# Attention stage of a decoder layer: the eight PSUM banks divided as five, two and one instead of four, two and two

## The chip, the cores and the metric

One core of a Trainium2 chip runs the whole kernel. The metric is the device time of one execution in microseconds; the median over the runs is compared. Of an execution taken by the hardware profiler there is also a trace with every instruction of every engine.

## What is computed

One decoder layer on a sequence of 2048 tokens of width 1024, in float32. The attention part, cut to what matters here:

```python
# banded heads: 8 query heads on 2 key heads of 64, window of 128 keys, a sink per head
out_a = sliding_window_sink_attention(qa, ka, va, sinks)
# differential heads: 4 heads, two causal softmax maps each, values of width 128
p = softmax(where(mask, q @ k.T * scale, -inf))      # for both maps c = 0, 1
a = p[:, :, 0] - lam * p[:, :, 1]
od = a @ v
out_b = rms_norm(od, g_diff) * (1.0 - lam_init)
x = x + concat(out_a, out_b) @ w_out
```

In front of it stand an RMS norm and one combined projection; behind it cross-attention to 256 memory tokens and a squared-ReLU MLP with 4096 hidden columns.

## The kernel before, in words

The layer is written as stages that follow each other: `phase_in` (norm, projections, rotary tables, L215), `phase_attention` (L435), `phase_out` (output projection, L768), then cross-attention (L813 to L1003) and the MLP (L1070 to L1218). Matrix products that need more than one pass split each float32 operand into a high and a low part and take three products.

The kernel uses PSUM as eight banks of 128x512 float32 values. `K.ps` (L87) takes a bank by a tag, and `BANKS` (L52) says how many buffers a tag has: four for `s`, two for `t`, two for `o`. One PSUM pool (L1246) serves the whole kernel. A tile keeps its bank until its last reader is done; the next tile of the tag waits for that.

The attention stage has four kinds of work, all in `phase_attention`.

- *Scores and exponentials of a unit* (`softmax`, L454). A unit is one differential head `h` and a block `s` of 256 queries: 4 heads by 8 blocks, 32 units. Keys are taken 512 at a time; for each such chunk and each half of the queries two maps are made. Two matmuls (L482) fill a bank of tag `s` (a third, L487, adds the causal mask in the last chunk), VectorE takes the negated row maximum (L488), ScalarE the exponential with that bias (L489) into an SBUF tile `p`. The exponential is the last reader of the bank.
- *Weighting* (`weigh`, L498). Small operations make each chunk's factors (L506 to L516). GpSimd multiplies the second map (L521), and VectorE computes first map times factor plus second (L528); for some tiles GpSimd does this too (L523, L524).
- *Values of a unit* (`values`, L533). For each 256 keys four transposes (L553) fill a bank of tag `t`. ScalarE copies it (L560), or ScalarE and VectorE split it into a high and a low part (L141, L142). Then matmuls with the values (L543) add into one bank of tag `o` that the unit holds from its first to its last matmul. At the end ScalarE copies it out (L571), GpSimd squares it (L572), and a sum over the partitions goes through a bank of tag `t` (L576, L578).
- *Banded heads* (`window_softmax`, L599, and `window_values`, L637). 32 pieces, each with two score banks of tag `s` (L611, read by L622 to L627), one bank of tag `t` for transposes (L643, L645), and one of tag `o` for the output `wo` (L657 to L663): two matmuls, and a copy by ScalarE.

Beside these, 16 columns of the memory's projection (`memory_column`, L752) run as filling: 24 matmuls into a bank of tag `t` and a split.

The order is written as a plan of times (L668 to L714). Each unit gets a start and a duration, from `U0` and `U1`; its score, weighting and value steps get planned times from `W0`, `W1` and `VL`. All steps are sorted by planned time and issued in that order (L713). A unit's value steps are planned behind its scores, by a formula (L693, L694) that takes no notice of the other units; where a unit follows a longer one, its first value step can be planned ahead of the last one's end. The units run over the blocks upward in heads 0 and 2 and downward in heads 1 and 3 (L39, L668). The program is built with a scheduler (L1328) that, per engine, puts an instruction whose inputs and buffers are there by its model ahead of one that still waits, with the written order as the priority; on the chip each engine then runs that fixed order.

The PSUM pool, like the SBUF pools, is opened with `reuse_waits="tile"` (L1241): a new tile waits for the earlier tiles at its place. The SBUF pool `work` (L1250) already takes over in this way the place of a pool that `phase_in` closes.

Of the kernel before, what the change touches and what calls it, by code (L numbers as in the profile page):

```python
# [9 lines left out]
F32 = mybir.dt.float32  # L10
# [7 lines left out]
P = 128  # L18
S = 2048
D = 1024  # L20
NT = S // P
# [15 lines left out]
W0, W1, VL, WS, WV = 2.0, 1.0, 4.0, (0.42, 0.6, 0.92), (0.33, 0.86)  # L37
# [11 lines left out]
AHEAD, WOUT = 3, 28  # L49

MAIN, STAGE, SLAB, W2, WIN, W2O = 36, 6, 4, 8, 5, 3
BANKS = dict(s=4, t=2, o=2)  # L52


SPLIT = ((1, 0, 1, 0, 1, 0, 1, 0), (1, 1, 1, 0, 1, 1, 1, 0), (1, 0, 0, 1, 0, 0, 1, 0))
# [2 lines left out]
def f(t):  # L58
    return t.bitcast(F32)
# [6 lines left out]
class K:  # L66
# [18 lines left out]
        return self.work_pool.tile(list(shape), dtype, name=name, tag="out", bufs=W2O)  # L85

    def ps(self, tag, shape=(P, 512), name="ps"):  # L87
        return self.psum_pool.tile(list(shape), F32, name=name, tag=tag, bufs=BANKS[tag])

    def bank(self, i, name="ps"):  # L90
        return self.ps("ssssttoo"[i], name=name)
# [111 lines left out]
def constants(k, pool):  # L203
    nc = k.nc
    k.ident = pool.tile([P, P], F32, name="ident")
    make_identity(nc, k.ident)
    k.identb = pool.tile([P, P], BF16, name="identb")
    nc.scalar.copy(k.identb, k.ident)
    k.gv = pool.tile([P, 48], F32, name="gv")
    k.load(k.gv, k.a["gvec"])  # L210
    k.g_mix, k.g_cross, k.g_mem, k.g_mlp, k.g_final = (k.gv[:, 8 * i : 8 * i + 8] for i in range(5))
    k.g_diff, k.inv_freq, k.sgn, k.qk_scale = (k.gv[:, 40 + i : 41 + i] for i in range(4))
# [222 lines left out]
def phase_attention(k, mt):  # L435

    nc = k.nc
    kv, sw, started, turned = {}, {}, {}, []
# [198 lines left out]
    def window_values(cc, g, b, p):  # L637

        vs = sw[cc, g][2]
        blk = 2 * cc + b  # L640
        tt = k.ps("t", [P, 4, P], name="wtt")
        for j in range(4):
            nc.tensor.transpose(tt[:, j, :], p[:, j], k.ident)  # L643
        a1 = k.win([P, 4, P], name="wa1")
        nc.scalar.copy(a1, tt)  # L645
        parts = [(b + 1, a1)]
        if blk:
            a0 = k.win([P, 4, P], name="wa0")
            nc.gpsimd.affine_select(
                out=a0, in_=a1, compare_op=ALU.is_ge, fill=0.0, base=-1, pattern=[[0, 4], [-1, P]], channel_multiplier=1  # L650
            )
            nc.gpsimd.affine_select(
                out=a1, in_=a1, compare_op=ALU.is_ge, fill=0.0, base=0, pattern=[[0, 4], [1, P]], channel_multiplier=-1
            )
            parts = [(b, a0), (b + 1, a1)]
        yield
        o = k.ps("o", [64, 512], name="wo")  # L657
        for x, (i, t) in enumerate(parts):
            nc.tensor.matmul(  # L659
                o, vs[:, i, :], t.rearrange("p a b -> p (a b)"), start=(x == 0), stop=(x == len(parts) - 1)  # L660
            )
        os_ = k.w2o([64, 4, P], name="wos")
        nc.scalar.copy(os_.rearrange("p a b -> p (a b)"), o)  # L663
        cs = slice(P * (blk % 4), P * (blk % 4) + P)
        nc.sync.dma_start(k.ow_d[blk // 4][:, 64 * g : 64 * g + 64, cs].rearrange("t f k -> f t k"), os_)
        yield
# [5 lines left out]
    def at(times, make, *args):  # L672

        state = []

        def step():
            if not state:
                state.append(make(*(y for x in args for y in (x[0] if isinstance(x, list) else (x,)))))
            return next(state[0], None)

        steps.extend((t, len(steps) + n, step) for n, t in enumerate(times))

    start = 0.0
    for i, (h, s) in enumerate(units):
        n, dur = (s + 2) // 2, U1 * (s + 1) + U0
        res = []

        def scores(h, s, i=i, res=res):
            yield from softmax(i, h, s, res)

        at([start + dur * (x + 0.5) / (2 * n) for x in range(2 * n)] + [start + dur * (1 - 0.1 / n)], scores, h, s)
        start += dur
        stt = [start + W0 + W1 * dur * (x + 1) / (2 * n) for x in range(2 * n)]  # L693
        val = [stt[2 * (x // 2) + 1] + VL + 0.5 * W1 * dur * (x % 2) / n for x in range(s + 1)]  # L694
        at([start] + stt, weigh, res)
        at(val + [val[-1] + VL, val[-1] + VL + 0.1], values, res)
    each = start / 32
    for i, win in enumerate(wins):
        res = []
# [44 lines left out]
def memory_load(k):  # L744
    mt = [[k.main([P, 4, MEM], name="mt") for _ in range(2)] for _ in range(2)]
    for y in range(2):
        for x in range(2):
            k.load(f(mt[x][y]), k.mt_d[x][y], chain="main")
    return mt
# [63 lines left out]
def cross_queries(k):  # L813

    nc, a = k.nc, k.a
    kk = [[k.main([P, 4, MEM], name="kk") for _ in range(2)] for _ in range(2)]
    for i in range(2):
        for x in range(2):
            k.load(f(kk[i][x]), k.kv_d[x][i], chain="main")
    wq = [[k.main(name="wq") for _ in range(2)] for _ in range(DT)]  # L820
    for h in range(4):
        pq = [k.bank(d, name="pq") for d in range(DT)]
        for e in range(2):
            w = k.slab2(a["w_cqT"][(2 * h + e) * P : (2 * h + e + 1) * P, :], "vector" if e else "gpsimd", h % 2 == 1)
            n = 2 * h + e
            for d in range(DT):
                for z, (s_, m_) in enumerate(((0, 0), (0, 1), (1, 0))):
                    nc.tensor.matmul(  # L828
                        pq[d][:, :256], w[s_][d // 4][:, P * (d % 4) : P * (d % 4) + P], kk[n // 4][m_][:, n % 4], start=(e == 0 and z == 0), stop=(e == 1 and z == 2)
                    )  # L830
        hs = slice(256 * h, 256 * h + 256)
        for d in range(DT):
            k.split(wq[d][0][:, hs], wq[d][1][:, hs], pq[d][:, :256], k.g_cross[:, d : d + 1])
    return wq
# [235 lines left out]
def phase_up(k, operands, rb, last_rstd):  # L1070
# [3 lines left out]
    def pair(half, n, sets, mid):  # L1074
# [23 lines left out]
        def add(ps, x, name, tile=k.w2):  # L1098
            t = tile(name=name)
            nc.vector.tensor_tensor(t, ps, x, op=ALU.add)  # L1100
            return t
# [119 lines left out]
def build(nc, tc, a, out):  # L1221
    k = K()
    k.last_load = {}
    k.nc, k.tc, k.a, k.out = nc, tc, a, out
    with ExitStack() as es:
        dp = es.enter_context(tc.tile_pool(name="dram", bufs=1, space=bass.MemoryType.DRAM))
        dram = lambda name, *shape: dp.tile(list(shape), F32, name=name)
        k.qk_d = [dram(f"qk_d{n}", 4 if n < 6 else 2, 2, HD, S) for n in range(7)]
        k.v_d = dram("v_d", 4, P, NT, 2 * P)
        k.vs_d = dram("vs_d", P, NT, P)  # L1230
        k.cs_d = dram("cs_d", 2, 32, S)
        k.ow_d, k.od_d = ([dram(f"{n}{i}", 4, P, 512) for i in range(4)] for n in ("ow_d", "od_d"))
        k.ss_d = [dram(f"ss_d{i}", 4, 512) for i in range(4)]
        k.rs_d = [dram(f"rs_d{i}", 1, 4, 512) for i in range(4)]
        k.kv_d = [[dram(f"kv_d{x}{i}", P, 4, MEM) for i in range(4)] for x in range(2)]
        k.mt_d = [[dram(f"mt_d{x}{i}", P, 4, MEM) for i in range(2)] for x in range(2)]
        k.t_d = [{n: dram(f"t_d{i}{n}", 2, 2, P, 512) for n in ("t1", "t2", "t3", "t4")} for i in range(2)]
        k.u_d = [[dram(f"u_d{c}_{n}", 2, P, 512) for n in range(16)] for c in range(4)]
        k.x1_d, k.x2_d = ([dram(f"{n}{c}", DT, P, 512) for c in range(4)] for n in ("x1_d", "x2_d"))

        pool = lambda name, **kw: es.enter_context(tc.tile_pool(name=name, bufs=1, reuse_waits="tile", **kw))  # L1241
        cp = pool("const")
        k.tiny_pool = pool("tiny")
        k.main_pool = pool("main")
        k.stage_pool = pool("stage")
        k.psum_pool = pool("psum", space=bass.MemoryType.PSUM)  # L1246
        constants(k, cp)
        k.rs1 = cp.tile([P, NT], F32, name="rs1")
        phase_in(k, cp)
        k.work_pool = pool("work")  # L1250
        started = phase_attention(k, memory_load(k))
        phase_out(k, started[WOUT])
        pt, last = cross_scores(k, cross_queries(k))
        vw = cross_values(k, last)
        operands = {}, {}
        make = mlp_operands(k, 0, operands[0])
        rb, last_rstd = cross_mix(k, pt, vw, lambda: [*mlp_combine(k, 0)], lambda: [next(make) for _ in range(4)])
        for _ in make:
            pass
        phase_up(k, operands, rb, last_rstd)  # L1260
        phase_down(k)
# [77 lines left out]
```

## Time and profile before

| | |
|---|---|
| median of 3 runs | 3046.49 us (3045.34 to 3056.3) |
| the profiled execution | 3047.63 us |
| its span, first to last instruction | 3045.6 us |
| granted TensorE clock, mean | 0.974 of full speed |
| busy share of the span | TensorE matmul 95%, weight load 77%, VectorE 58%, ScalarE 37%, GpSimd 38% |

How to read it: the profile page gives each engine's busy share over the whole span, and that mixes stages. Every part of the argument on the attention stage needs rows of that stage alone: busy time in a window, waits in that window, instructions in order of time. A wait is put down to the instruction that released it. Clock 1.00 is the 2.4 GHz level, 0.50 the 1.2 GHz level.

### The profile page before, as it was taken

What the parts mean: (1) busy time and instruction counts of PE and PEld (TensorE: products, weight loads), DVE (VectorE), ACT (ScalarE), POOL (GpSimd) and SP (SyncE); (2) the same over time, 40 slices, a digit from 0 to 9 for tenths busy, and PEclk for the clock granted to TensorE, in tenths of its full rate; (3) what the DMA queues carried; (4) which work ended last, traced back from release to release, by engine and by line L of the source; (5) the groups of instructions that cost most, each with busy time, mean ns of one, the idle gap of its engine ahead of it and who ended that gap; (6) DMA issues with size and microseconds to landing.
All of it is one profiled execution on the core that took longest, in us unless ns stands there. A gap on an engine that the chain in (4) does not pass through costs nothing.

```text
span 3045.6 us, 38727 instructions
## 1 busy us (share of the span) xinstructions
PE 2884.5 (95%) x13740; PEld 2350.0 (77%) x13740; DVE 1760.0 (58%) x2918; ACT 1125.9 (37%) x2481; POOL 1163.8 (38%) x914
## 2 busy tenths in 40 slices
PE   8999989989999899999995999989999999999996
PEld 8978866666666688888883877878888888888886
DVE  5254448887788642423345756665556566656656
ACT  7221137666767422444223333433342111111113
POOL 0133336765676542112124666665561101110115
PEclk9999989989999999999997999999999999999997
DMA  8443363434432664211327345443346122212203
GB/s 310 133 178 126 111 197 115 121 84 140 126 109 81 196 208 138 84 42 66 108 90 276 124 148 170 145 154 111 111 139 228 63 76 77 77 63 77 77 7 111
DMA packets 223297, 380.21 MB, mean 125 GB/s; under 512 B 25313, under 2 KB 95105, under 8 KB 223105
## 3 DMA queue, kind: packets, MB, share of 16 engines
q1 hardware_dynamic: 223104, 377.75, 37.5%
q8 instruction: 108, 1.77, 0.2%
q14 instruction: 85, 0.69, 0.1%
HBM read 259.65 MB, written 116.98 MB: 124 GB/s over the span
## 4 chain that ended last, share of the span: by engine, by line
PE 61%; DVE 5%; DMA 4%; POOL 4%; issue 2%; ACT 1%; SPq 0%; POOLq 0%; DVEq 0%; ACTq 0%
PE pd L1179 23%; PE p L1093 15%; PE po L804 6%; PE sc L868 6%; PE po L992 5%; PE sc L482 1%; DMA xs<-x_d 1%; DVE p L528 1%; PE o L543 1%; POOL w L1089 1%; PE wo L659 1%; DMA wf<-w_up 1%; PE pv L934 1%; PE pq L828 1%; POOL p L521 1%
## 5 line engine op out<-in xcount | busy, mean ns | idle before, releaser
L1093 PE MATMUL p<-xh,w 128*128 128x512 f32 x1792 | 557.3, 392 | 42.9 <-ACT w L1088 27.6
L1183 DVE TENSOR_TENSOR acc<-pd,acc 128x512 f32<-128x512 f32 (+1 forms) x520 | 351.2, 681 | 253.7 <-PE pd L1179 251.2
L1093 PEld LDWEIGHTS p<-xh,w 128*128 128x128 f32 x1792 | 337.0, 189 | 121.3 <-ACT w L1088 29.6
L1179 PE MATMUL pd<-uh,wdh 128*128 128x512 f32 (+1 forms) x1040 | 401.7, 386 | 1.0 <-DVE acc L1183 1.0
L1179 PE MATMUL pd<-ul,wdh 128*128 128x512 f32 (+1 forms) x1040 | 401.2, 386 | 0.0
L1179 PE MATMUL pd<-uh,wdl 128*128 128x512 f32 (+1 forms) x1040 | 401.2, 386 | 0.0
L1093 PE MATMUL p<-xl,w 128*128 128x512 f32 x896 | 350.3, 391 | 0.0
L117 POOL TENSOR_TENSOR wdl<-wf,wdh 128x1024 fp32r<-128x1024 f32 x32 | 78.0, 2440 | 549.6 <-ACT wdh L116 543.8
L489 ACT ACTIVATE p<-sc,nm 128x512 f32<-128x512 f32 (+3 forms) x320 | 198.8, 627 | 95.9 <-DVE nm L488 94.3
L482 PE MATMUL sc<-kt,q 128*128 128x512 f32 (+2 forms) x640 | 199.1, 414 | 32.0 <-ACT p L489 22.4
L1179 PEld LDWEIGHTS pd<-uh,wdh 128*128 128x128 f32 x1040 | 195.3, 188 | 40.4 <-DVE acc L1183 1.2
L1179 PEld LDWEIGHTS pd<-ul,wdh 128*128 128x128 f32 x1040 | 195.3, 188 | 39.4
L1179 PEld LDWEIGHTS pd<-uh,wdl 128*128 128x128 f32 x1040 | 195.3, 188 | 39.3
L488 DVE TENSOR_REDUCE nm<-sc 128x1 f32<-128x512 f32 (+3 forms) x320 | 184.3, 601 | 51.5 <-PE sc L487 29.4
L1093 PEld LDWEIGHTS p<-xl,w 128*128 128x128 f32 x896 | 169.1, 189 | 35.2
L482 PEld LDWEIGHTS sc<-kt,q 128*128 128x128 f32 x640 | 108.7, 199 | 84.4 <-ACT p L489 43.4
L521 POOL TENSOR_TENSOR p<-p,scl 128x512 f32<-128x512 f32 (+3 forms) x144 | 151.6, 1081 | 55.0 <-DVE scl L516 50.2
L141 ACT CAST uh<-uf 128x1024 fp32r<-128x1024 f32 x64 | 65.8, 1049 | 276.2 <-PE pd L1179 263.7
L303 PE MATMUL pa<-hh,wh 128*128 128x512 f32 x416 | 162.7, 391 | 0.0
L303 PE MATMUL pa<-hl,wh 128*128 128x512 f32 x416 | 162.5, 391 | 0.0
L303 PE MATMUL pa<-hh,wl 128*128 128x512 f32 x416 | 162.1, 390 | 0.0
L172 POOL TENSOR_TENSOR tot<-tot,sq 128x512 f32<-128x512 f32 x56 | 77.5, 1384 | 207.8 <-ACT sq L171 206.1
(266 smaller groups left out, 6051.8 us busy)
## 6 DMA issues: line engine op xcount, KB each, us to landing
wf<-w_up SPq DMA_DIRECT2D x64, 512.0 KB
u_d<-u SPq DMA_DIRECT2D x128, 256.0 KB
uf<-u_d SPq DMA_DIRECT2D x64, 512.0 KB
qk_d<-rot SPq DMA_DIRECT2D x96, 256.0 KB
x_d<-x SPq DMA_DIRECT2D x32, 512.0 KB
x<-x_d SPq DMA_DIRECT2D x32, 512.0 KB
xs<-x_d SPq DMA_DIRECT2D x32, 512.0 KB
wf<-w_down SPq DMA_DIRECT2D x32, 512.0 KB
```

Of the source, the lines that this page charges most:

```text
L117: getattr(nc, eng).tensor_tensor(lo, wf, f(hi), op=ALU.subtract)
L303: nc.tensor.matmul(pa, s_[d // 4][:, P * (d % 4) : P * (d % 4) + P], hs(m_, c, d), start=(d == 0 and i == 0), stop=(d == DT - 1 and i == 2),)
L482: mm = nc.tensor.matmul(sc[:, :um], q[:, x, c, P * t : P * t + P], kt[:, c, :um], start=(x == 0), stop=(x == 1 and not last))
L488: nc.vector.tensor_reduce(nm[:, t, j, c : c + 1], sc[:, :u], axis=AX.X, op=ALU.max, negate=True)
L489: nc.scalar.activation(p[:, c, :u], sc[:, :u], AF.Exp, bias=nm[:, t, j, c : c + 1], accum_out=l[:, t, j, c : c + 1])
L521: nc.gpsimd.tensor_tensor(p[:, 1, :u], p[:, 1, :u], sc[:, t, j, 1:2].broadcast_to([P, u]), op=ALU.mult)
L804: nc.tensor.matmul(po, wo[d][s_][:, P * n : P * n + P], m_[d // 2][:, d % 2], start=(d == 0 and z == 0), stop=(d == 7 and z == 2))
L868: nc.tensor.matmul(sc[n], x[s_][d][:, ts], wq[d][m_][:, 512 * n : 512 * n + 512], start=(d == 0 and z == 0), stop=(d == DT - 1 and z == 2))
L992: nc.tensor.matmul(po[i], vw[b][s_][:, P * n : P * n + P], m_[b], start=(b == 0 and z == 0), stop=(b == 7 and z == 2))
L1093: nc.tensor.matmul(ps, t[:, s_, P * d : P * d + P], x[d][m_], start=(d == 0 and z == 0), stop=(d == 3 and z == 2))
L1179: nc.tensor.matmul(pd, w[ft][s_][:, P * n : P * n + P], u[m_][:, ft, ts], start=(ft == 0 and z == 0), stop=(ft == 1 and z == 2))
L1183: nc.vector.tensor_tensor(av, pd, av, op=ALU.add)
```

## The change

In the attention stage the tags get five, two and one banks: a fifth bank for scores (`s`), two for `t`, and only one for values (`o`). The banded heads' output `wo` moves from tag `o` to tag `t`. To this end the PSUM pool is opened three times, for `phase_in`, for attention, and for the rest. The plan of times gets a running `done`: a unit's value steps are planned no earlier than the end of the values of the unit before. All other work is the same.

```diff
--- before.py
+++ after.py
@@ -49,7 +49,7 @@
 AHEAD, WOUT = 3, 28
 
 MAIN, STAGE, SLAB, W2, WIN, W2O = 36, 6, 4, 8, 5, 3
-BANKS = dict(s=4, t=2, o=2)
+BANKS, BANKS_ATTENTION = dict(s=4, t=2, o=2), dict(s=5, t=2, o=1)
 
 
 SPLIT = ((1, 0, 1, 0, 1, 0, 1, 0), (1, 1, 1, 0, 1, 1, 1, 0), (1, 0, 0, 1, 0, 0, 1, 0))
@@ -85,7 +85,7 @@
         return self.work_pool.tile(list(shape), dtype, name=name, tag="out", bufs=W2O)
 
     def ps(self, tag, shape=(P, 512), name="ps"):
-        return self.psum_pool.tile(list(shape), F32, name=name, tag=tag, bufs=BANKS[tag])
+        return self.psum_pool.tile(list(shape), F32, name=name, tag=tag, bufs=self.banks[tag])
 
     def bank(self, i, name="ps"):
         return self.ps("ssssttoo"[i], name=name)
@@ -654,7 +654,7 @@
             )
             parts = [(b, a0), (b + 1, a1)]
         yield
-        o = k.ps("o", [64, 512], name="wo")
+        o = k.ps("t", [64, 512], name="wo")
         for x, (i, t) in enumerate(parts):
             nc.tensor.matmul(
                 o, vs[:, i, :], t.rearrange("p a b -> p (a b)"), start=(x == 0), stop=(x == len(parts) - 1)
@@ -680,7 +680,7 @@
 
         steps.extend((t, len(steps) + n, step) for n, t in enumerate(times))
 
-    start = 0.0
+    start = done = 0.0
     for i, (h, s) in enumerate(units):
         n, dur = (s + 2) // 2, U1 * (s + 1) + U0
         res = []
@@ -691,9 +691,14 @@
         at([start + dur * (x + 0.5) / (2 * n) for x in range(2 * n)] + [start + dur * (1 - 0.1 / n)], scores, h, s)
         start += dur
         stt = [start + W0 + W1 * dur * (x + 1) / (2 * n) for x in range(2 * n)]
-        val = [stt[2 * (x // 2) + 1] + VL + 0.5 * W1 * dur * (x % 2) / n for x in range(s + 1)]
+        val = []
+        for x in range(s + 1):
+            done = max(done, stt[2 * (x // 2) + 1] + VL + 0.5 * W1 * dur * (x % 2) / n)
+            val.append(done)
+        done += VL
         at([start] + stt, weigh, res)
-        at(val + [val[-1] + VL, val[-1] + VL + 0.1], values, res)
+        at(val + [done, done + 0.1], values, res)
+        done += 0.2
     each = start / 32
     for i, win in enumerate(wins):
         res = []
@@ -1243,12 +1248,21 @@
         k.tiny_pool = pool("tiny")
         k.main_pool = pool("main")
         k.stage_pool = pool("stage")
-        k.psum_pool = pool("psum", space=bass.MemoryType.PSUM)
-        constants(k, cp)
-        k.rs1 = cp.tile([P, NT], F32, name="rs1")
-        phase_in(k, cp)
+
+        def psum(scope, banks):
+            k.banks = banks
+            k.psum_pool = scope.enter_context(tc.tile_pool(name="psum", bufs=1, reuse_waits="tile", space=bass.MemoryType.PSUM))
+
+        with ExitStack() as scope:
+            psum(scope, BANKS)
+            constants(k, cp)
+            k.rs1 = cp.tile([P, NT], F32, name="rs1")
+            phase_in(k, cp)
         k.work_pool = pool("work")
-        started = phase_attention(k, memory_load(k))
+        with ExitStack() as scope:
+            psum(scope, BANKS_ATTENTION)
+            started = phase_attention(k, memory_load(k))
+        psum(es, BANKS)
         phase_out(k, started[WOUT])
         pt, last = cross_scores(k, cross_queries(k))
         vw = cross_values(k, last)
```

## Rows read from the trace of the kernel before

**Rows 1.** Busy time in a stretch: its us; PE, PEld, DVE, ACT, POOL; clock; DMA.
```profile
425.00:1035.00 610.00, 545.74 (x2983) 394.73 (x2983) 493.11 (x1026) 410.14 (x1261) 379.41 (x383) 0.95 0.41 121
```

**Rows 2.** TensorE's waits, 425 to 1035 us: us in total, times, longest us.
```profile
PE sc L482 <- ACT p L489: 22.4, 27, 2.5
PE o L543 <- DVE al L142: 7.7, 8, 2.4
...
PE sc L482 <- ACT wp L627: 4.5, 6, 1.9
PE tt L553 <- DVE al L142: 4.2, 2, 2.4
PE sc L482 <- DMA q<-qk_d: 3.1, 4, 1.2
PE o L543 <- ACT af L560: 3.1, 3, 1.3
PE o L543 <- ACT ah L141: 3.1, 3, 1.7
PE tt L553 <- DVE kv L142: 2.7, 2, 1.6
PE wsc L611 <- ACT p L489: 1.5, 2, 1.1
```

**Rows 3.** Timeline around one stall: start us, us, engine, line [idle before it].
```profile
567.17 0.68 ACT L489 ACTIVATE p<-sc,nm 128x512 f32<-128x512 f32 x1
...
567.32 0.73 PE L482 MATMUL sc<-kt,q 128*128 128x512 f32 x2 [0.42 <-ACT p L489]
...
568.55 1.19 DVE L528 SCALAR_TENSOR_TENSOR p<-p,scl 128x512 f32<-128x512 f32 x1
...
569.67 1.28 DVE L488 TENSOR_REDUCE nm<-sc 128x1 f32<-128x512 f32 x2
570.38 0.69 ACT L489 ACTIVATE p<-sc,nm 128x512 f32<-128x512 f32 x1 [2.18 <-DVE nm L488]
...
571.21 2.08 PE L482 MATMUL sc<-kt,q 128*128 128x512 f32 x4 [2.49 <-ACT p L489]
```

**Rows 4.** VectorE's waits, 425 to 1035 us: us in total, times, longest us.
```profile
DVE nm L488 <- PE sc L487: 29.4, 31, 3.1
DVE nm L488 <- PE sc L482: 20.8, 24, 2.3
```

**Rows 5.** Busy time in three stretches with a lower clock, columns as in rows 1.
```profile
570.00:580.00 10.00, 7.00 (x12) 2.49 (x12) 10.00 (x16) 5.41 (x20) 9.90 (x10) 0.50 0.03 12
...
660.00:670.00 10.00, 7.75 (x30) 5.04 (x30) 5.88 (x16) 5.79 (x19) 1.47 (x2) 0.66 0.10 29
680.00:690.00 10.00, 7.44 (x23) 3.88 (x21) 8.55 (x20) 4.59 (x15) 7.33 (x8) 0.66 0.51 135
```

**Rows 6.** Groups by line, 425 to 1035 us: xcount | busy us, mean ns | idle before.
```profile
L528 DVE SCALAR_TENSOR_TENSOR p<-p,scl 128x512 f32<-128x512 f32 (+3 forms) x112 | 129.8, 1176 | 3.4 <-POOL p L521 3.3
...
L553 PE MATMUL tt<-ident,p 128*128 128x128 f32 x560 | 89.1, 284 | 12.3 <-DVE p L528 4.7 <-DVE al L142 4.2 <-DVE kv L142 2.7
...
L659 PE MATMUL wo<-wa,wv 128*64 128x512 f32 x124 | 68.1, 644 | 1.2 <-POOL wa L649 1.1
...
L560 ACT COPY af<-tt 128x512 f32<-128x512 f32 (+1 forms) x80 | 45.0, 563 | 17.5 <-PE tt L553 17.0
L142 DVE TENSOR_TENSOR al<-tt,ah 128x512 fp32r<-128x512 f32 x64 | 43.7, 682 | 12.3 <-ACT ah L141 12.0
...
L141 ACT CAST ah<-tt 128x512 fp32r<-128x512 f32 x64 | 37.2, 583 | 8.3 <-PE tt L553 8.3
...
L663 ACT COPY wos<-wo 64x512 f32<-64x512 f32 x32 | 18.4, 574 | 4.4 <-PE wo L659 3.5 <-ACT p L489 0.8
```

**Rows 7.** First matmul of the output projection, then the copies from value banks.
```profile
L804 PE MATMUL po<-oh,woh x39: 387/389/499, 1031.9 to 1059.9; 128*128 128x512 f32 x39
...
L571 ACT COPY os<-o x32: 356/377/427, 440.9 to 1039.1; 128x256 f32<-128x256 f32 x32
```

## Prediction

> **What bounds the kernel now.** The change touches only the attention stage, so I first read a table of busy time over a window that leaves out the stage's slow first microseconds, 425 to 1035 us. There TensorE is busy 545.7 of 610 us, VectorE 493.1, ScalarE 410.1 and GpSimd 379.4, at a mean granted clock of 0.95 [rows 1]. No engine is full: TensorE stands idle for 610 − 545.7 = 64 us, VectorE for 117 us. The stage is several engines handing work to each other, and it loses time where one is late. What a change here can give is bounded by these idle times and by the clock.
>
> Second, the list of what TensorE waits for in that window. The largest entry is a score matmul (L482) waiting for ScalarE's exponential (L489): 22.4 us in 27 waits, the longest 2.5 us. With the same wait behind a banded head's exponential (L627), 4.5 us in 6, and the banded scores' own wait, 1.5 us in 2, that is 28.4 us in 35 waits [rows 2]. The exponential is the last reader of a score bank, so these are waits for a free bank of the four. The next group, 7.7 + 3.1 + 3.1 us of value matmuls (L543) waiting for split or copied weights, isn't about banks at all. Waits for a transpose bank (transposes behind the second half of a split, L142) are 4.2 and 2.7 us [rows 2]. No wait on a value bank (for the copy of L571 or L663) is in the list.
>
> Third, one such stall in order of time. A pair of score matmuls starts at 567.32 us (0.73 us for the pair). The exponential that would free the next bank starts only at 570.38, because it waited 2.18 us for a maximum that VectorE started at 569.67, behind two long weighting operations (1.19 us the second). TensorE then waits 2.49 us, until 571.21 [rows 3]. So the stall is made by VectorE's order and speed; TensorE runs out of banks while it lasts.
>
> Fourth, VectorE's own waits: it waits 29.4 and 20.8 us, in 31 and 24 waits, for scores to arrive [rows 4]. Sometimes scores are early and find no bank, sometimes late and find VectorE idle: that is what more buffers smooth.
>
> **The change part by part.**
>
> *A fifth score bank.* In the stall of [rows 3] the bank freed by the exponential of 567.17 (0.68 us) would have been the fifth, so the pair of 571.21 would have started some 2 us earlier, and the one behind it would have met the same late exponential. One burst of waits therefore gives back about one pair, 0.73 us, not the whole stall. If each of the 35 waits were a burst of its own, that is 35 × 0.73 = 26 us; if three belong to a burst, 12 × 0.73 = 8.8 us. The bounds are 8.8 us and all 28.4 us. The mean wait, 28.4 / 35 = 0.81 us, is close to one pair, so most single waits would fit in the lead of one pair; I take the middle, 19 us.
>
> *VectorE's waits for scores.* The order on each engine is made when the program is built, for the banks that there are, so scores can also be placed earlier. That can shorten the 50.2 us of [rows 4]. Much of it is the same time as above seen from the other side: between 0 and 50.2 us, I take 4.
>
> *The clock.* Behind stalls the granted clock falls: 0.50 in 570 to 580 us (the 1.2 GHz level for the whole stretch), 0.66 in 660 to 670 and in 680 to 690, where TensorE was busy only 7.0 to 7.75 of 10 us [rows 5]. That is 5.0 + 3.4 + 3.4 = 11.8 us of full-speed work lost. Some of it is hidden, since in 570 to 580 VectorE is busy for 10.0 of 10 us. I take 5, between 0 and 11.8.
>
> *Banded outputs (wo) in the transpose banks.* 32 tiles move from the value banks to the two transpose banks. Each holds a bank for its matmuls (68.1 / 32 = 2.1 us) and its copy (18.4 / 32 = 0.57 us), 2.7 us, 86.5 us in all. The main tenants' transposes, copies and splits take 89.1 + 45.0 + 37.2 + 43.7 = 215 us [rows 6], so their load on these banks grows by 0.4 of itself. The present waits for such a bank are 4.2 + 2.7 = 6.9 us [rows 2]. Taking waits as the square of the load, 1.4² is about 2: it costs another 7 us. The lower end is 0, as in the list today these waits are few. The upper end is every wo delaying a transpose by its whole hold, 32 × 2.7 = 86 us.
>
> *One value bank, values one by one.* The bank passes from unit to unit 31 times. The hand-over is one copy on ScalarE, 0.38 us [rows 7], plus what stands ahead of it there, at most about one exponential (0.69 us, [rows 3]). The plan now starts a unit's values no sooner than the last unit's are done; by its formulas 24 of the 31 hand-overs move, by 0.4 to 5.4 of a plan that is 366 units long. Transposes and their copies need no value bank, so TensorE has those and the scores to do meanwhile. The nearest row is a value matmul that waits for a copy of transposes, 3.1 + 3.1 + 7.7 us over 144 such steps, 0.10 us each [rows 2, 6]. I take that: 31 × 0.1 = 3 us. The ends are 0 and 31 × (0.38 + 0.69) = 33 us. Against this stands the Trainium skill, Perfetto Trace Analysis, section Matmuls: independent groups of matmuls should rotate through banks, so that reading one out overlaps the next. By that rule the hand-over is exposed and the sum would have 33 in place of 3. The trace doesn't show which, as two banks serve there.
>
> *Opening and closing the pools.* At the end of attention the first matmul of the output projection starts at 1031.9 us, and the last copy from a value bank is at 1039.1 [rows 7]. If a closing pool held back all that follows, that overlap of 7.2 us would be lost. The pool is declared to wait by tile, and the output projection takes score banks, which are long free: I take 0, and keep 7.2 for the upper end. No instruction is added, and no DMA. A slab of weights waits for its transposes up to 5.4 plan units longer, so loads that reuse its place may come later; score matmuls wait for loaded queries 3.1 us in 4 waits now [rows 2]. I take 0, and at most as much again, 3.1.
>
> **The sum.** −19 − 4 − 5 + 7 + 3 = −18 us. The profiled execution took 3047.63 us (a span of 3045.6 with 2 us around it), 1.1 us above the median of 3046.49. So the forecast is 3047.6 − 18 − 1.1 = 3028.5, say 3028 us.
>
> **The rivals.**
> - *VectorE sets the pace, and a bank doesn't change it: no difference.* In [rows 3] the stall is a queue of weighting operations (L528) ahead of the maximum. They take 1176 ns on average, at 128x512 and smaller, where a split of 128x512 takes 682 [rows 6], and VectorE is at 10.0 of 10 us in [rows 5]. If it is the limit whenever TensorE stalls, only the one pair per burst of three is left, and neither the clock nor VectorE's waits change: −8.8 + 7 + 3 = +1, 3047 to 3048 us. For it speaks that every stall I followed leads to VectorE; against it, the 50 us for which VectorE waits for scores. Beside this: the Trainium skill, SBUF — State Buffer, section Who interferes with whom, says that a VectorE instruction with two inputs in SBUF contends with a GpSimd instruction that reads SBUF. L528 is of that kind and L142 is not, and the two means agree with it. This would happen whatever the banks.
> - *The transpose banks become the narrow place: slower.* wo, the memory columns, the row sums and both kinds of transposes then share two banks. If half of the wo tiles delay a transpose by their whole hold, 16 × 2.7 = 43 us, the sum is 43 + 3 − 28 = +18, 3064 us. It decides from about (28 − 3) / 2.7 = 9 of 32 tiles on. For it: these banks already show waits of up to 2.4 us [rows 2]. Against: there are 4 of them, and a fifth score bank gives TensorE other work.
> - *The value bank's hand-over is exposed.* All 31 at 1.07 us give 33 + 7 − 28 = +12, 3058 us: still within the noise, but no gain. For it: TensorE takes its instructions in a fixed order, so what stands behind the waiting value matmul waits too. Against: the order is made with one bank in view. The rule on Matmuls above is this mechanism.
>
> **How the numbers follow.** Forecast 0.44, VectorE's pace 0.28, transpose banks 0.17, value bank 0.11. About 0.5%, 15 us, is what a measurement of this kernel can tell from no change. The forecast stands just beyond that on the fast side. VectorE's pace counts as same, and so does the value bank but for 0.04 where several copies wait for more than one exponential. So faster 0.44, same 0.28 + 0.07 = 0.35, slower 0.17 + 0.04 = 0.21. The range's low end takes the whole of the bank waits and of the clock, VectorE's 4, and no cost: 3046.5 − 28.4 − 11.8 − 4 = 3002, so 3002. Its high end is 3060: it holds the value bank's case and leaves out most of the transpose banks' case. What is left out is that and a tail of larger gains below, about 0.2. The forecast's own range is 3002 to 3031.
>
> **What would show it.** Right: score matmuls waiting for L489 and L627 fall from 28 to about 10 us, VectorE's waits for scores fall a little, the granted clock of the window is above 0.95, and the list of TensorE's waits shows transposes behind the copy of wo (L663) and value matmuls behind L571 with single microseconds. For VectorE's pace: score waits hardly fall, or turn into waits of transposes and values for VectorE. For the transpose banks: transposes behind L663, L578 and L142 with tens of us. For the value bank: L543 behind L571. The forecast is wrong if the window is not shorter while the score waits are gone, since then they weren't what ended last.

## The result, and the profile after

The changed kernel takes 3120.4 us (median of 4, 3118.46 to 3121.06) against 3045.9: the ratio is 1.0237 with an interval of 1.0213 to 1.026. It is slower by 74 us, where I forecast 18 us less. The range, 3002 to 3060, doesn't hold it.

The whole loss lies between the first scores and the output projection. Busy time in that stretch after the change (stretch in us; its length; PE, PEld, DVE, ACT, POOL busy; granted clock; DMA share; GB/s), and in its last 50 us:

```profile
425.00:1103.00 678.00, 572.00 (x2969) 401.40 (x2969) 498.60 (x1029) 422.17 (x1268) 384.04 (x387) 0.92 0.37 113
1050.00:1100.00 50.00, 34.91 (x149) 23.33 (x149) 28.32 (x45) 26.79 (x49) 20.46 (x15) 0.81 0.55 187
```

The engines do the same work as in [rows 1], VectorE 499 us against 493 and GpSimd 384 against 379, but it takes 678 us and not 607 (the first matmul of the output projection was at 1031.9 in [rows 7]). TensorE's idle time goes from 64 to 106 us, and its busy time from 546 to 572 us for about as many matmuls: the lower clock costs 0.08 × 678 = 54 us of full speed against 0.05 × 610 = 30. So about 42 us more are waits, and about 26 us are a lower clock.

What ends when: last exponential of a score (L489) in the kernel before, and then in the changed one.

```profile
L489 ACT ACTIVATE p<-sc,nm x320: 342/687/754, 428.2 to 1009.5; 128x512 f32<-128x512 f32 x112, 128x128 f32<-128x128 f32 x16, 128x256 f32<-128x256 f32 x16, 128x384 f32<-128x384 f32 x16
```

```profile
L489 ACT ACTIVATE p<-sc,nm x320: 342/687/780, 426.5 to 1049.4; 128x512 f32<-128x512 f32 x112, 128x128 f32<-128x128 f32 x16, 128x256 f32<-128x256 f32 x16, 128x384 f32<-128x384 f32 x16
```

The last copy from a value bank and the first matmul of the output projection in the changed kernel (its L809 is L804 of before):

```profile
L571 ACT COPY os<-o x32: 362/373/438, 436.9 to 1100.0; 128x256 f32<-128x256 f32 x32
```

```profile
L809 PE MATMUL po<-oh,woh x256: 387/389/795, 1102.6 to 1281.3; 128*128 128x512 f32 x128
```

So 40 us of the loss come before the last exponential (1009.5 to 1049.4). Behind it, before, 29.6 us passed until the last value was copied out, now 50.6: 21 us more, with TensorE busy 34.9 of 50 us. And the output projection no longer overlaps with the last values, as in [rows 7], but follows them: another 10 us.

TensorE's waits after the change, from 425 to 1103 us (total, times, longest):

```profile
PE sc L482 <- ACT p L489: 44.4, 46, 3.4
PE o L543 <- DVE al L142: 14.4, 12, 4.6
PE pss L576 <- POOL os L572: 11.1, 10, 2.4
PE sc L482 <- DMA q<-qk_d: 6.3, 9, 1.7
...
PE sc L482 <- ACT wp L627: 5.3, 9, 1.3
...
PE wsc L611 <- ACT p L489: 3.0, 7, 1.0
...
PE tt L553 <- DVE al L142: 1.6, 4, 0.9
```

With one bank more the waits for a score bank have gone from 28.4 us [rows 2] up to 44.4 + 5.3 + 3.0 = 52.7. Waits for a transpose bank are fewer, not more, and value matmuls waiting for the last unit's copy (L571) aren't in the list: neither sign that I had named for the two rivals on banks shows. The row sum (pss, L576) waiting for its square on GpSimd has grown to 11.1 us. Before the change it was (425 to 1035 us):

```profile
PE pss L576 <- POOL os L572: 0.8, 1, 0.8
```

VectorE's waits for scores haven't fallen either (50.2 us in [rows 4]). Its largest entry is now its half of the split waiting for ScalarE's half, 34.9 us against 12.0 in [rows 6]:

```profile
DVE al L142 <- ACT ah L141: 34.9, 18, 7.3
DVE nm L488 <- PE sc L487: 34.3, 29, 3.3
DVE nm L488 <- PE sc L482: 22.2, 25, 2.9
```

What happens between two units can be followed at one hand-over, the one from unit 15 to unit 16 of the 32. The changed kernel in order of time (start us, us, engine, line [idle before it]):

```profile
768.53 4.27 POOL L521 TENSOR_TENSOR p<-p,scl 128x512 f32<-128x512 f32 x4 [7.86 <-DMA ow_d<-wos]
...
769.72 0.38 ACT L571 COPY os<-o 128x256 f32<-128x256 f32 x1
...
772.76 1.49 POOL L523 TENSOR_TENSOR p<-p,scl 128x512 f32<-128x512 f32 x1
...
774.80 0.91 POOL L572 TENSOR_TENSOR os<-os 128x256 f32<-128x256 f32 x1
...
776.71 2.08 PE L482 MATMUL sc<-kt,q 128*128 128x512 f32 x4 [2.61 <-ACT p L489]
...
778.71 1.01 PE L576 MATMUL pss<-os,ones 128*1 128x256 f32 x2
...
779.65 0.61 PE L553 MATMUL tt<-ident,p 128*128 128x128 f32 x3
...
785.10 0.38 ACT L571 COPY os<-o 128x256 f32<-128x256 f32 x1
```

The unit's values are copied out at 769.72. The square that follows (L572) stands in GpSimd's queue behind weighting for other units and starts at 774.80. When it is done, at 775.71, TensorE stands at score matmuls (L482) that wait for an exponential and come first in its order. The row sum comes at 778.71, and only then, at 779.65, the first transposes of the next unit: 9.9 us behind the copy. The next unit's values are copied out 15.4 us after this unit's. I went through all 31 hand-overs in the trace by the start times of the copy (L571), the row sum (L576) and the first copy of the next unit's transposes (L560 or L141). Before, that first copy comes on average 1.0 us after the value copy, in 19 cases ahead of it, and behind the row sum in 9. After, it comes 6.4 us after the value copy, never ahead of it, and behind the row sum in all 31. In the plan the row sum is part of a unit's last step, and the next unit's first step now always comes later.

This hand-over is a long one. On average the square starts 1.5 us after the copy's end (1.4 before), and the row sum 3.7 us after the copy's start (4.5 before). The row sum comes no later than it did; what changed is that the next unit's transposes now stand behind it. Nor is the 6.4 us the loss. From one value copy to the next it takes 21.4 us on average, before 19.3: the part from a unit's first copy of transposes to its value copy has become shorter, 15.0 us for 18.3.

### The profile page after: what moved, and what is told of

Same layout as the page of the kernel before. It is cut to its first block, busy times and chain, and to the rows that moved or that the text cites. A ratio compares the mean times of both kernels' runs of the same rounds, so it can differ in the third digit from the quotient of the medians.

```text
span 3116.7 us, 38745 instructions
## 1 busy us (share of the span) xinstructions
PE 2913.2 (93%) x13740; PEld 2358.5 (76%) x13740; DVE 1755.1 (56%) x2918; ACT 1130.8 (36%) x2481; POOL 1163.0 (37%) x914
## 4 chain that ended last, share of the span: by engine, by line
PE 56%; DMA 3%; POOL 2%; DVE 2%; issue 1%; ACT 0%; SPq 0%; POOLq 0%; DVEq 0%; ACTq 0%
PE pd L1184 22%; PE p L1098 16%; PE po L809 6%; PE sc L873 6%; PE po L997 5%; DMA xs<-x_d 1%; POOL w L1094 1%; DMA wf<-w_up 1%; PE pv L939 1%; PE pq L833 1%; PE pt L901 0%; DVE xs L1030 0%; PE col L181 0%; POOL o L1172 0%; DMA t_d1t<-xs 0%
## 5 line engine op out<-in xcount | busy, mean ns | idle before, releaser
L482 PE MATMUL sc<-kt,q 128*128 128x512 f32 (+2 forms) x640 | 206.7, 423 | 56.4 <-ACT p L489 44.4
L489 ACT ACTIVATE p<-sc,nm 128x512 f32<-128x512 f32 (+3 forms) x320 | 199.2, 630 | 115.7 <-DVE nm L488 114.4
L482 PEld LDWEIGHTS sc<-kt,q 128*128 128x128 f32 x640 | 110.2, 202 | 100.9 <-ACT p L489 67.9
L141 ACT CAST uh<-uf 128x1024 fp32r<-128x1024 f32 x64 | 65.8, 1049 | 275.9 <-PE pd L1184 263.7
```

Source lines behind the costliest of these rows:

```text
L482: mm = nc.tensor.matmul(sc[:, :um], q[:, x, c, P * t : P * t + P], kt[:, c, :um], start=(x == 0), stop=(x == 1 and not last))
L489: nc.scalar.activation(p[:, c, :u], sc[:, :u], AF.Exp, bias=nm[:, t, j, c : c + 1], accum_out=l[:, t, j, c : c + 1])
```

## The experiments

The changed kernel differs from the one before in five things. The first runs take them one by one.

**pools_422.** Only the three pools; four, two, two banks, wo in `o`, old plan.

```diff
-BANKS, BANKS_ATTENTION = dict(s=4, t=2, o=2), dict(s=5, t=2, o=1)
+BANKS, BANKS_ATTENTION = dict(s=4, t=2, o=2), dict(s=4, t=2, o=2)
```

> The PSUM pool opened three times, all else as before (four, two, two; wo in the value banks; old plan). All theories but one expect no difference: 3040 to 3052 us. If closing and opening the pool is what costs, 3100 us or more.

3053.6 us, ratio 1.0022 (1.0013 to 1.0031). Slightly outside what I expected: 7.2 us. They lie where the pool closes. Here are its output projection's first matmul and its last copy from a value bank:

```profile
L807 PE MATMUL po<-oh,woh x256: 387/389/795, 1039.5 to 1217.6; 128*128 128x512 f32 x128
```

```profile
L571 ACT COPY os<-o x32: 351/376/426, 439.8 to 1036.1; 128x256 f32<-128x256 f32 x32
```

The values end earlier than in [rows 7] (1036.1, before 1039.1), and the projection starts 7.6 us later, behind them.

**wo_t_422.** As pools_422, and wo moved to the transpose banks.

> Four, two, two, old plan, only wo moved to the transpose banks. Theory 'one value bank' (units hand the only bank over one after the other; values fall behind, the last ones stand alone at the end): within 15 us of before, 3035 to 3060. Rival 'transpose banks too full': most of the 74 us, 3090 us or more.

3072.6 us, 1.0089 (1.0074 to 1.0104): 19 us above pools_422. Between the two theories.

**plan_422.** As pools_422, with the new plan only (the `done` lines of the diff).

> Four, two, two, wo in the value banks, only the new plan, in which a unit's values are planned behind the last unit's. Theory 'one value bank': two banks still overlap, within 15 us of before, 3035 to 3060. Rival 'the plan': the later value steps alone cost most of it, 3090 us or more.

3084.3 us, 1.0126 (1.011 to 1.0143): 31 us above pools_422, with two value banks. Also between. At the hand-overs it looks like the changed kernel: the next unit's first copy comes 6.0 us after the value copy, behind the row sum in all 31.

**b421.** The changed kernel with `s=4`, one bank unused.

> The changed kernel with four score banks instead of five, one bank unused (four, two, one; wo in the transpose banks; new plan). Theory 'one value bank': as slow as the changed kernel or slower, 3115 to 3135 us. Rival 'the fifth score bank lets scores run ahead and does the harm': near before, 3040 to 3070 us.

3112.8 us, 1.0216 (1.0199 to 1.0232). The fifth score bank doesn't do the harm; without it 66 of the 74 us remain. Nor does it do any good here: with it the kernel is 8 us slower. VectorE's half of the split waits less for ScalarE's half than in the changed kernel (425 to 1090 us):

```profile
DVE al L142 <- ACT ah L141: 14.2, 17, 2.8
```

**b422_both.** The changed kernel with `s=4, t=2, o=2`: both moves, and two value banks.

> Four, two, two with wo in the transpose banks and the new plan: the changed kernel but for one bank that goes from scores to values. Theory 'single file in the plan' (it is the order of the value steps that costs, whether one bank or two): 3100 to 3118 us, as with one value bank (3113). Rival 'the one value bank itself': the second bank lets units overlap again, 3070 to 3095 us.

3108.2 us, 1.0203 (1.0183 to 1.0223). So the number of value banks isn't the cause: under this plan the second one gives back some 4 us of 66 (3112.8 to 3108.2), and the intervals of the two ratios overlap. What is left is the order. (One value bank needs such an order: by the old plan's formulas 20 of the 31 following units would take a value bank before the unit ahead is copied out. No run tries that.)

Step by step from the kernel before, on these runs, the 74 us are 7.2 for the pools (pools_422), 54.7 for wo and the plan together (b422_both), 4.5 for the second value bank taken away (b421) and 7.6 for the fifth score bank (the changed kernel).

**late_pss.** The changed kernel with the row sum as a step of its own, planned 2.9 units of the plan's time later; the square stays with the copy. (The whole plan has 366 such units, so they are not the 32 units of work. At some 607 us for the stage, 2.9 of them are about 5 us: an estimate.)

```diff
         nc.sync.dma_start(k.od_d[s // 2][h, :, cs], os_[:, 0])
+        yield
         pss = k.ps("t", [1, 256], name="pss")
...
-        at(val + [done, done + 0.1], values, res)
+        at(val + [done, done + 0.1, done + 3.0], values, res)
```

> The changed kernel (five, two, one), with each unit's row sum (square, sum over partitions) planned 3 units of the plan later, so that it no longer stands ahead of the next unit's transposes. If the row sum at the hand-over is a main part of the loss: 3090 to 3108 us. If the rest of the chain (last matmul, copy, then the next unit's transposes, copies, matmuls) is: 3112 to 3125 us.

3046.5 us, 0.9993 (0.9981 to 1.0005). One step moved, and all 74 us are back, far more than I expected. The stretch of the stage is as long as before the change (columns as above):

```profile
425.00:1030.00 605.00, 538.58 (x2976) 395.04 (x2975) 484.85 (x1027) 410.48 (x1265) 381.60 (x386) 0.96 0.41 124
```

The same hand-over as above, from unit 15 to unit 16, in late_pss:

```profile
741.78 0.49 PE L553 MATMUL tt<-ident,p 128*128 128x128 f32 x3
741.79 0.36 ACT L571 COPY os<-o 128x256 f32<-128x256 f32 x1
...
743.10 0.69 POOL L572 TENSOR_TENSOR os<-os 128x256 f32<-128x256 f32 x1
...
746.19 0.59 PE L577 MATMUL pss<-os,ones 128*1 128x256 f32 x2
...
748.29 0.36 ACT L571 COPY os<-o 128x256 f32<-128x256 f32 x1
```

The next unit's transposes now stand ahead of the square and the row sum, and its own values are copied out 6.5 us after the last ones (15.4 in the changed kernel). Over the 31 hand-overs the next unit's first copy comes 1.9 us after the value copy, and in 3 cases behind the row sum. From value copy to value copy it takes 19.0 us on average.

**ov521.** The value bank taken only at a unit's first matmul, its first transposes planned ahead of the last matmuls of the unit before, the row sum 1.9 units of the plan later.

> Five, two, one, with the value bank taken only at a unit's first matmul, the first transposes of the next unit planned ahead of the last matmuls of this one, and the row sum 2 units later. Theory 'single file': the chain at each hand-over is cut, at least half of 58 us comes back, 3060 to 3092 us. Rivals 'transpose banks' or 'scores running ahead': little comes back, 3105 us or more.

3059.0 us, 1.004 (1.0026 to 1.0053). Below my interval by 1 us, so 61 us come back. With more overlap than late_pss (22 of 31 first copies ahead of the value copy) it is slower than that.

**b322.** As pools_422 with three score banks.

> Three pools, old plan, wo in the value banks, three score banks instead of four (three, two, two). What the fourth bank is worth: if scores are short of banks as the prediction has it (0.73 us a burst for each bank), 3070 us or more against 3053 with four. If VectorE sets the pace, 3045 to 3062 us.

3103.3 us, 1.0186 (1.0165 to 1.0206): the fourth score bank is worth 50 us in the old order. Scores do depend on banks, up to four.

**b421_late.** late_pss with four score banks.

> As late_pss (3046) but four score banks, one bank unused. What the fifth score bank is worth once the row sum is late. By the prediction's sum the fifth bank gives 19 + 5 + 4 us: 3065 to 3080 us. Rival 'VectorE sets the pace': 3040 to 3052 us.

3046.4 us, 0.9997 (0.9986 to 1.0008): the fifth score bank is worth nothing in this order, 3046.4 against 3046.5. TensorE's waits, and VectorE's for ScalarE's half of the split, show where it went. First late_pss with five banks (425 to 1030 us), then b421_late with four (425 to 1027):

```profile
PE o L543 <- DVE al L142: 21.0, 14, 6.5
PE sc L482 <- ACT p L489: 9.9, 15, 2.1
PE sc L482 <- DMA q<-qk_d: 5.9, 6, 1.6
...
PE o L543 <- ACT af L560: 3.0, 3, 1.5
...
PE sc L482 <- ACT wp L628: 0.2, 1, 0.2
```

```profile
DVE al L142 <- ACT ah L141: 16.7, 15, 4.0
```

```profile
PE sc L482 <- ACT p L489: 18.2, 24, 2.2
PE o L543 <- DVE al L142: 10.6, 11, 4.5
PE sc L482 <- ACT wp L628: 6.2, 8, 1.3
```

```profile
DVE al L142 <- ACT ah L141: 7.1, 11, 1.3
```

With the fifth bank the waits of L482 for a score bank fall from 24.4 to 10.1 us, about as I had forecast. But value matmuls wait for VectorE's split (L142) 21.0 us in place of 10.6. The wait has only changed its name. It doesn't end at VectorE, though: VectorE's half of the split itself waits for ScalarE's half, 16.7 us in place of 7.1. The same entry grows with the fifth bank in the early order too, from 14.2 us in b421 to 34.9 in the changed kernel.

**before_late.** The kernel before (one pool, four, two, two, old plan), with the row sum 2.9 units of the plan later.

> The kernel before (four, two, two, one pool, old plan) with the row sum 3 units of the plan later, and nothing else. If the row sum's place only matters where units go in single file: 3040 to 3052 us. If it holds up the transposes there too: 3020 to 3037 us.

3038.7 us, 0.9972 (0.9962 to 0.9981): a little faster than both kernels, just outside what I expected of either.

**pss_s.** The changed kernel with the row sum's bank from `s` instead of `t`.

> The changed kernel (five, two, one) with the row sum's bank taken from the score banks instead of the transpose banks; its planned time stays as changed, right behind the unit's copy. Theory 'the row sum holds the queue for a transpose bank' (its bank is asked for ahead of the next unit's transposes, and they wait for it): most comes back, 3045 to 3070 us. Rival 'its place in the plan alone': little comes back, 3105 us or more.

3073.8 us, 1.009 (1.0068 to 1.0113): 47 of 74 us come back with no change of the plan. The trace shows that the next unit's transposes get past the row sum this way: their first copy comes 2.1 us after the value copy, and behind the row sum in 8 cases. So asking for a transpose bank ahead of the next unit goes with a large part of the harm, but not with all.

**single_late.** late_pss with one pool of five, two, one for the whole kernel.

> As late_pss, but with one PSUM pool of five, two and one for the whole kernel (the eight-bank stages take their fifth bank from the score banks), so that no pool is closed. If the closing pools cost 7 us as in pools_422: 3034 to 3043 us. Rival: the stages with one bank for sums and transposes lose it again, 3044 us or more.

3059.5 us, 1.0041 (1.0028 to 1.0054): slower than late_pss. Where it loses is open; that it is in the other stages isn't shown.

**b431.** The changed kernel with `s=4, t=3, o=1`.

> The changed kernel (wo in the transpose banks, new plan, row sum at its place) with four, three and one banks: one bank goes from scores to transposes. Theory 'the row sum holds the queue for a transpose bank': with a third one the next unit's transposes get a bank beside it, 3045 to 3075 us. Rival 'one unit after the other in the plan': no change, 3100 us or more.

3082.1 us, 1.0111 (1.0093 to 1.0129). Outside both expectations: against b421 the third transpose bank gives back 31 of 66 us. But it doesn't do so in the way that I expected. The next unit's first copy still comes 6.0 us after the value copy (6.1 in b421), behind the row sum in all 31, and TensorE waits at the row sum no less. Here is b431 (425 to 1071 us), and then b421 (425 to 1090):

```profile
PE pss L576 <- POOL os L572: 13.1, 9, 3.7
PE sc L482 <- DMA q<-qk_d: 5.9, 8, 1.8
```

```profile
PE pss L576 <- POOL os L572: 11.6, 9, 4.0
PE sc L482 <- DMA q<-qk_d: 11.2, 11, 2.6
```

What fell are score matmuls' waits for loaded queries, among others. So the 31 us don't speak for a row sum that holds the queue for a bank.

**wo_t_late.** wo_t_422 with the row sum 2.9 units of the plan later.

> wo_t_422 (3073; four, two, two, three pools, old plan, wo in the transpose banks) with the row sum 3 units later. If wo costs only as one more that queues for a transpose bank behind a waiting row sum: 3040 to 3056 us. If wo itself fills the banks: 3064 us or more.

3052.7 us, 1.0014 (1.0002 to 1.0026). The 19 us of wo_t_422 are gone, and it is no slower than pools_422 (3053.6). So wo alone doesn't fill the banks. That the row sum is what it meets there isn't shown. Here is TensorE's wait at the row sum in pools_422 (425 to 1045 us), and then in wo_t_422 (425 to 1061):

```profile
PE pss L576 <- POOL os L572: 6.8, 4, 4.6
```

```profile
PE pss L576 <- POOL os L572: 6.2, 6, 1.5
```

**late_out.** late_pss with `phase_out` inside the attention's pool.

> late_pss (3046) with the output projection inside the attention's PSUM pool, so that the pool is closed one stage later. If closing a pool with work behind it costs 7 us at the start of the output projection: 3036 to 3042 us. Rival: the cost only moves to the next stage, 3044 to 3050 us.

3045.3 us, 0.9991 (0.9982 to 1.0): near the edge, and the rival has it. The output projection's and the next stage's first matmul, in late_out and then in late_pss:

```profile
L810 PE MATMUL po<-oh,woh x256: 387/389/499, 1025.9 to 1207.7; 128*128 128x512 f32 x128
```

```profile
L834 PE MATMUL pq<-kk,wh x128: 277/283/415, 1212.3 to 1241.1; 128*128 128x256 f32 x128
```

```profile
L810 PE MATMUL po<-oh,woh x256: 387/389/628, 1030.2 to 1208.2; 128*128 128x512 f32 x128
```

```profile
L834 PE MATMUL pq<-kk,wh x128: 278/283/385, 1208.9 to 1234.9; 128*128 128x256 f32 x128
```

The projection starts 4.3 us earlier, and the stage after it 3.4 us later: in these two executions the cost of closing moves to the next border.

**before_late6** and **before_late15.** before_late with the row sum at 6.0 and at 1.5 units of the plan instead of 3.0.

> before_late (3039) with the row sum 6 instead of 3 units later. If the row sum only had to get out of the way: 3035 to 3042 us. If the later sum holds its output tile too long: 3043 us or more.

> before_late (3039) with the row sum 1.5 instead of 3 units later. If any place a little behind the copy does: 3035 to 3042 us. If 3 is what fits: between 3039 and the 3046 of the kernel before, or above.

3065.1 us, 1.0051 (1.0032 to 1.0071), and 3046.6 us, 1.0006 (0.9993 to 1.0019). The gain of before_late is there at one of three distances, so it is a fit to this order rather than a rule. The 3065.1 lies in the range for a later sum that holds its output tile too long. ScalarE does wait there for stores of output tiles, 4.5 + 3.2 + 3.0 = 10.7 us against 2.4 in before_late; whether that makes the difference isn't shown.

**late03.** late_pss with the row sum 0.25 units later in place of 2.9.

> The changed kernel with the row sum planned just 0.25 units of the plan later, which puts it behind the next unit's first transposes where these are planned right at the hand-over, and no further. If only its turn ahead of those transposes for a bank matters: 3045 to 3070 us, near late_pss (3046). If it needs the distance, so that the square is done when TensorE gets there: 3085 to 3120 us.

3100.0 us, 1.0182 (1.0166 to 1.0197): 20 us come back, the rest doesn't. That is the range for the case that the row sum needs the distance. Its last exponential, its last value copy and the head of TensorE's waits (425 to 1087 us):

```profile
L489 ACT ACTIVATE p<-sc,nm x320: 357/687/786, 428.4 to 1051.3; 128x512 f32<-128x512 f32 x112, 128x128 f32<-128x128 f32 x16, 128x256 f32<-128x256 f32 x16, 128x384 f32<-128x384 f32 x16
```

```profile
L571 ACT COPY os<-o x32: 352/373/438, 437.6 to 1084.7; 128x256 f32<-128x256 f32 x32
```

```profile
PE sc L482 <- ACT p L489: 35.8, 39, 2.9
PE sc L482 <- DMA q<-qk_d: 12.5, 10, 3.2
```

The values now end 33.4 us after the last exponential, as in late_pss (994.2 and 1027.6), and no longer 50.6. That gives 17 us; the two profiled executions are 15 us apart (3118.46 and 3103.15), the medians 20. The next unit's first copy comes 2.7 us after the value copy, close to late_pss, and in 8 cases behind the row sum. But what is won there is mostly lost again inside the unit: from its first copy to its value copy it takes 18.1 us on average, 15.0 in the changed kernel and 17.1 in late_pss. From value copy to value copy it takes 20.9 us, for 21.4 and 19.0. And the last exponential is as late as in the changed kernel, 1051.3.

## Why the prediction was wrong

Of the 92 us between 18 us faster and 74 slower, 45 are the plan and wo, 36 the fifth score bank, 7 the pools and 4.5 the second value bank.

**The step that failed** first is the one on the value bank and the values one by one. I priced the hand-over as one copy on ScalarE, 0.1 us each by the nearest row and 1.07 at most, and wrote that "transposes and their copies need no value bank, so TensorE has those and the scores to do meanwhile". They do need no value bank, and a second value bank is worth only some 4 us (b422_both against b421). But the plan put them behind the last unit's row sum, in all 31 hand-overs, and that needs a square on GpSimd. I followed the copy's readers as far as ScalarE and missed the row sum, though the listing of the code shows it in the same step. Measured: the plan alone 31 us (plan_422), against 3 in the sum; plan and wo together 55 (3108.2 less 3053.6), against 3 + 7. My upper ends, 33 for the hand-overs and 86 for wo, did hold the 31 and wo's 19. That is luck: the 33 was made of copies on ScalarE, and no wait for that copy is in the list.

**wo in the transpose banks.** I took 7 us, and it cost 19 (wo_t_422). With the row sum late it costs nothing (wo_t_late), so it isn't the load that I had worked out. My slower rival had these banks as the narrow place. The waits that it named didn't grow to tens of us, and a third transpose bank gives back 31 us without moving the next unit ahead of the row sum (b431). What wo met is open.

**The fifth score bank.** I took 19 + 4 + 5 us of gain. With the row sum late it is worth 0, with the row sum early it costs 8. This is the second step that failed: I took a wait that gets shorter for time that is won. The waits for a bank fell to the level I forecast (late_pss), but they came back as waits of value matmuls for VectorE's split, which the rival "VectorE sets the pace" had named as its sign. That VectorE is the pace isn't shown, since it waits there for ScalarE's half itself. b322 shows that the same argument would have been right one bank lower: 50 us from three to four.

**The clock** went the other way, together with TensorE's idle time: 54 us lost against 30.

**The pools.** I took 0 and kept 7.2 for the upper end. It cost 7.2 (pools_422), by the overlap that I had named. For loaded queries I took 0 and at most 3.1; TensorE's waits for them went from 3.1 to 6.3 us.

**The rule on Matmuls** (the Trainium skill, Perfetto Trace Analysis, section Matmuls: independent groups should rotate through banks) had the sign right for the kernel. As a price it isn't borne out here: with the row sum late, one value bank takes 3046 us (late_pss), as two did before. b422_both doesn't test it: its two banks could rotate, but its plan keeps the units in single file.

What is shown: the place of the row sum carries the loss. Moving it alone by 2.9 units of the plan takes back 74 us (late_pss against the changed kernel), 66 (b421_late against b421) and 20 (wo_t_late against wo_t_422), and 8 in the kernel before. What is not shown is the way by which it costs. That it holds the queue for a transpose bank agrees with pss_s (47 of 74), but b431 gains without it and late03 gets past it and gains only 20. The gap at the hand-over doesn't follow the time either: 6.0 us in plan_422 (3084 us), 6.0 in b431 (3082), 6.1 in b421 (3113), 2.7 in late03 (3100). No run takes the square off GpSimd, so GpSimd's part isn't measured by itself. And the order of every engine and of the loads' queue is made anew for each version; no run separates that from the row sum's distance to its square.

## What to carry to other kernels

When work is put in single file, list every instruction of the step that closes one item, through all engines to its last reader, and look which of them stands ahead of the next item's first instruction. Here the place of a small row sum was worth 74 us, and the second value bank some 4. A long wait was worth no buffer here, and it came back at the next engine; one run with a buffer less and one with a buffer more tell that before anything else is changed. And a gap between two items is not yet a loss: measure from the end of one to the end of the next.

## What I had not expected of the hardware and the program

The value of a bank falls very steeply: 50 us from the third to the fourth score bank (old order), nothing from the fourth to the fifth (new order, row sum late). And the order that is made at build time is so sensitive that the row sum's place at 1.5, 3 and 6 plan units gives 3046.6, 3038.7 and 3065.1 us with the same work. That is a spread of 26 us. Differences of that size between two orders of this stage, as wo's 19 us and the fifth bank's 8, shouldn't be read as the worth of the edit that made them unless a second pair of runs says the same.
